# Next pair's input transposes ahead of an overflow conditional, and spilled rows gathered one pair ahead

## The chip, the cores and the metric

The kernel is one program on one core of a Trainium2 chip. The metric is the device time of one execution in microseconds (us); less is better. A core has a matrix engine (TensorE, PE in the rows; PEld is its weight load), VectorE (DVE), ScalarE (ACT), GpSimd (POOL) and SyncE (SP), each with its own instruction stream, and sixteen DMA engines that move data between HBM and on-chip memory. The engines wait for each other through semaphores.

## What is computed

The reference is a two-layer trunk over 512 latent and 256 context tokens of width 1024. Layer 0 mixes tokens with a 2-D Fourier transform and a convolution, layer 1 with two kinds of attention. Each layer ends in a mixture of experts: every token picks one of four groups and in it two of eight experts. Nearly all that the change touches is this part:

```python
def routed_experts(h, e_idx, e_w, w_gate, w_up, w_down):
    ...
    xb = h_pad[row_tok].reshape(n_blocks, EXPERT_BLOCK, d)
    def expert_block(args):
        xblk, e = args
        return (jax.nn.silu(xblk @ w_gate[e]) * (xblk @ w_up[e])) @ w_down[e]
    ...
    return jnp.zeros((n_tok + 1, d), h.dtype).at[row_tok].add(yb * row_w[:, None])[:n_tok]
```

with d = 1024, 32 experts, an expert width of 512, everything in float32. Layer 0 routes 768 tokens (latent and context), layer 1 only the 512 latent ones.

## The kernel before

The program is unrolled: a mixer phase, the experts of layer 0 (`moe`, about 313 to 885 us of the profile), the attention phase, and the experts of layer 1 (about 1266 to 1815 us). In each expert stage all 32 experts are worked off as 16 pairs, in the order ORDER = 0..15.

**A pair.** Each expert of a pair has room for 64 tokens, one half of a 128-row tile. `gather` (L1212) fetches the pair's token rows from HBM into `xg` by an indirect DMA that POOL issues; an index that lies beyond the bound is skipped. `xpose` transposes `xg` on PE (8 instructions, `ps<-cst,xg` in the rows) and ACT and DVE copy the result to `xt`. Then, for the first expert, `gate_up` (16 matmuls of each 4 of the 8 slices, `psg<-ring,mk`), `gated` (Silu on ACT L1338, two products on DVE L1340), `turned` (two transposes, `ps<-cst,hb`), `down` (16 matmuls, `ps<-ring,hb`) and `place` (ACT L1369 copies the result to `y`); the same for the second expert, whose accumulator is `other`. `combine` adds the previous pair's outputs to the stream in between (`ps<-mk,mk`).

**The conditional.** A pair in which an expert got more than 64 tokens needs `overflow` (L1473): behind `tc.If(spills > 0)` stand two inner conditionals (L1477) that run a second half block for one expert from the pair's own `xt`, and one more (L1479) for rows that fit in neither half ("spilled" rows): `spill_gather` (L1381) fetches them into `xs`, and `spill_block`, `spill_split` and `spill_combine` work them off; L1494 is a conditional behind these for still more of them. All engines test the same condition, each in its own stream. An engine that does not enter jumps over the code and then brings its semaphore counters to the values that the others expect; until it has, whoever waits for that engine waits.

**The order around it.** PE's instructions and the weight loads on SP stand in program order by hand. The rest is ordered by the framework's scheduler, which also carries matmuls that are written behind the conditional up ahead of it where nothing forbids that: from the third pair on the `gate_up(other, ..., range(4, 6))` written behind `overflow` stands ahead of the branch.

**The weights.** Six tiles of 2 MB per pair (2048 KB in the rows) go through a ring of eight slots. `load(4)` behind the conditional issues four of them on SP, `load(1)` behind the last `gate_up` of the second expert and `load(1)` behind its `down` one each. A load waits until its slot's last reader on PE is done.

Of the kernel before, what the change touches and what calls it, by code (L numbers as in the profile page):

```python
# [12 lines left out]
ALU = mybir.AluOpType  # L13
# [3 lines left out]
P = 128  # L17
D = 1024
KD = D // P
# [25 lines left out]
ORDER = tuple(range(16))  # L45
# [16 lines left out]
class Kern:  # L62
# [804 lines left out]
    def moe(self, l, segs, outp, rt, last=False):  # L867
        self.turn = 7 - l
        nc, tc, A = self.nc, self.tc, self.A
        V, S, T, G = nc.vector, nc.scalar, nc.tensor, nc.gpsimd  # L870
# [6 lines left out]
        with ExitStack() as es:  # L877
# [333 lines left out]
            def gather(pr_):  # L1211
                return G.indirect_dma_start(  # L1212
                    out=xg, out_offset=None, in_=h2d,
                    in_offset=bass.IndirectOffsetOnAxis(ap=idi[:, pr_:pr_ + 1], axis=0),
                    bounds_check=n, oob_is_err=False)
# [74 lines left out]

            def spill_cols(f, i, pq, w):
                V.tensor_reduce(f[:, 0], pq[:, 0:2 * w].rearrange("p (h e) -> p e h", h=2), axis=AX.X, op=ALU.add)
                V.tensor_copy(i[:, 0], f[:, 0])
                V.tensor_scalar(f[:, 0], f[:, 0], -1.0, None, op0=ALU.add)
                V.tensor_reduce(f[:, 1], third(pq[:, 2 * w:5 * w]), axis=AX.X, op=ALU.add)

# [2 lines left out]
            def spill_table():  # L1299
                spill_cols(sf, si, spill_ids(None, slice(0, 160)), 32)  # L1300
# [30 lines left out]
            def gate_up(po, W, xt, s, ks):  # L1331
                for k in ks:
                    for c in range(2):
                        T.matmul(po[64 * c:64 * c + 64, :], xt[:, k, s], W[0](k // 4)[:, k % 4, c, :], start=k == 0, stop=k == KD - 1)
# [20 lines left out]
            def down(W, ht):  # L1355
                pd = self.ps()
                for j, kt in enumerate((0, 2, 1, 3)):
                    for dh in range(2):
                        T.matmul(pd[64 * dh:64 * dh + 64, :], ht[kt % 2][:, 64 * (kt // 2):64 * (kt // 2) + 64],
                                 W[1]()[:, kt, 512 * dh:512 * dh + 512], start=j == 0, stop=j == 3)  # L1360
                return pd

            def place(dst, i, pd, add=True):
                for dh in range(2):
                    d, p = dst[64 * i:64 * i + 64, 512 * dh:512 * dh + 512], pd[64 * dh:64 * dh + 64, :]
                    if add:
                        V.tensor_tensor(d, p, d, op=ALU.add)  # L1367
                    else:
                        S.activation(d, p, AF.Copy)  # L1369

            def combine(ms, yh, yl, sel):
                for m in ms:
                    pss = [self.ps() for _ in segs]
                    for z, y in enumerate((yh, yl)):
                        for p, (o, w) in zip(pss, segs):
                            T.matmul(p[:, :w], y(m), sel(m)[:, o:o + w], start=z == 0, stop=z == 1)
                    for v, (p, (o, w)) in enumerate(zip(pss, segs)):
                        self.add_gated(m, p, o, w, gate, v)

            def spill_gather(e, ids):  # L1380
                G.indirect_dma_start(  # L1381
                    out=xs[half(e % 2)], out_offset=None, in_=h2d,
                    in_offset=bass.IndirectOffsetOnAxis(ap=ids[0:64], axis=0),
                    bounds_check=n, oob_is_err=False)

            def spill_sel(so, h, idc):
                V.tensor_scalar(so[h], self.cst[h, K_IOTA:K_IOTA + n], idc[h], None, op0=ALU.is_equal)
# [81 lines left out]
            def overflow(pos_, pr_, Ws, xt, y, ys):  # L1469
                shared[0] = {}  # L1470
                if pos_ % 8 == 0:
                    spills[:] = nc.values_load_multi_w_load_instructions(nbi[0:1, 2, 16 + pos_:24 + pos_])[1]
                with tc.If(spills[pos_ % 8] > 0, label=f"ov{l}_{pr_}"):  # L1473
                    tc.mark_branch_hint_location(f"sp{l}_{pr_}", "LikelyTaken", [mybir.EngineType.PE])
                    for i in range(2):
                        e = 2 * pr_ + i
                        with tc.If(value(1, e, None) > 0):  # L1477
                            place(y, 1 - i, extra(Ws[i], xt, half(1 - i), wd[:, 1 - i, e:e + 1]), i == 1)
                    with tc.If(value(3, pr_, None) > 0, label=f"sp{l}_{pr_}"):  # L1479
                        rs_ = [value(0, 2 * pr_ + i, 12) for i in range(2)]  # L1480
                        so = keep([n], F32R, tag="S")
                        for i in range(2):
                            e = 2 * pr_ + i
                            spill_gather(e, si[:, 0, e:e + 1])
                            clear(i, *ys)
                            spill_sel(so, half(i), sf[:, 0, e:e + 1])
                        for i in range(2):
                            e = 2 * pr_ + i
                            with tc.If(rs_[i] > 0):
                                parts = spill_block(Ws[i], e, sf[:, 1, e:e + 1])  # L1490
                                spill_split(e, parts, *ys)
                        spill_combine(slice(0, P), so, *ys)
                        for i in range(2):
                            with tc.If(rs_[i] > 1):  # L1494
                                spill_rest(2 * pr_ + i, Ws[i], rs_[i] - 1, ys)
                shared[0] = None
# [9 lines left out]
            for p, r_ in enumerate(ORDER):  # L1506
                y = keep([D], tag="y3", bufs=3)
                ys = [keep([D], F32R, tag="y3", bufs=3) for _ in range(2)]
                G.memset(y[64:128], 0.0)  # L1509
                W = weights(p)  # L1510
                tc.mark_branch_hint_location(f"ov{l}_{r_}", "LikelyTaken", [mybir.EngineType.PE])
                gate_up(pa, W[0], xt, half(0), range(4, KD))
                h = gated(pa, wd[:, 0, 2 * r_:2 * r_ + 1])
                other = self.bank()
                gate_up(other, W[1], xt, half(1), range(2))
                ht = turned(h)
                if p == 0:
                    spill_table()
                if pend:
                    combine(range(4), *pend)  # L1520
                gate_up(other, W[1], xt, half(1), range(2, 4))
                if pend:
                    combine(range(4, KD), *pend)
                place(y, 0, down(W[0], ht), False)
                overflow(p, r_, W, xt, y, ys)
                load(4)
                if p == 15 and not last:
                    early = []
                    for q in range(2):
                        a = slot()  # L1530
                        for j in range(2):
                            pin(nc.sync.dma_start(out=a[:, 2048 * j:2048 * j + 2048].rearrange("p (k n) -> p k n", k=2), in_=A["modw"][1, 2, 2 * q + j]))
                        early += [a[:, D * k:D * k + D] for k in range(4)]
                gate_up(other, W[1], xt, half(1), range(4, 6))
                own = xt
                if p < 15:
                    xt = xpose(xg, slice(0, P), "xt", 2)
                    if p < 14:
                        gather(ORDER[p + 2])
                gate_up(other, W[1], own, half(1), range(6, KD))  # L1540
                load(1)
                h = gated(other, wd[:, 1, 2 * r_ + 1:2 * r_ + 2])
                if p < 15:
                    pa = self.bank()
                    nw = weights(p + 1)[0]
                    gate_up(pa, nw, xt, half(0), range(2))
                ht = turned(h)
                if p < 15:
                    gate_up(pa, nw, xt, half(0), range(2, 4))
                place(y, 1, down(W[1], ht))  # L1550
                load(1)
                yh, yl = ys
                for q in range(2):
                    cs_ = slice(512 * q, 512 * q + 512)
                    S.activation(yh[:, cs_], y[:, cs_], AF.Copy)  # L1555
                    V.tensor_tensor(yl[:, cs_], y[:, cs_], yh[:, cs_], op=ALU.subtract)  # L1556
                sel = keep([n], F32R, tag="S")
                V.tensor_scalar(sel, self.cst[:, K_IOTA:K_IOTA + n], idf[:, r_:r_ + 1], None, op0=ALU.is_equal)  # L1558
                pend = ((lambda m, a=yh: a[:, mc(m)]), (lambda m, a=yl: a[:, mc(m)]), (lambda m, a=sel: a))
# [135 lines left out]
```

## Time and profile before

| | |
|---|---|
| time, median of 3 runs | 1827.63 us (1825.91 to 1828.39) |
| profiled execution | 1831.84 us, of which the span is 1830.1 us |
| PE busy | 1650.3 us (90%) |
| DVE / ACT / POOL busy | 938.0 / 479.7 / 254.1 us |
| moved by DMA | 507.62 MB, mean 277 GB/s |
| mean granted TensorE clock | 0.958 |

The span runs from the first instruction to the last; the 1.74 us between it and the profiled execution's time lie around it. Engine names with a q (ACTq) are an engine's sequencer: a wait "<-ACTq L1473" ended when ACT's stream had passed the conditional of line 1473. In a row of the timeline the idle time ahead of the instruction stands in brackets, with what ended it. [...]

### The profile page before, as it was taken

The numbers are of one execution on the slowest core, as the hardware profiler recorded it, in microseconds if no ns is written. First come the engines' busy times: TensorE is split into PE (matmuls) and PEld (weight loads), VectorE is DVE, ScalarE is ACT, GpSimd is POOL, SyncE is SP. The second block draws the span as 40 slices with busy tenths as digits, with TensorE's granted clock in tenths as the row PEclk, the third lists the DMA queues.
The fourth block names the chain that finished last, engine by engine and source line by source line (L and its number), as shares of the span: only waits on it lengthen the run. The fifth ranks groups of instructions, "written<-read, shape, count | busy, mean of one in ns | idle before, by whom it ended". The sixth has DMA issues, their size and how long they took to land. (4 is left out here: it accounts for less than half of the span.)

```text
span 1830.1 us, 23551 instructions
## 1 busy us (share of the span) xinstructions
PE 1650.3 (90%) x8877; PEld 915.9 (50%) x8877; DVE 938.0 (51%) x1738; ACT 479.7 (26%) x1044; POOL 254.1 (14%) x200
## 2 busy tenths in 40 slices
PE   6998997989999987999799899997979899999896
PEld 4776785433343433444386778775323333333332
DVE  5799867333353533444555876555223333324235
ACT  4211632111111111111444555342112111111112
POOL 1231343000000010000232201121000000000001
PEclk8999998999999998999999999998999999999998
DMA  8876164778799992999422122376868979989972
GB/s 292 282 241 235 47 276 149 320 315 358 312 418 390 427 353 78 398 425 427 170 65 66 44 87 59 126 269 274 358 275 365 423 324 426 411 346 426 428 306 104
DMA packets 62062, 507.62 MB, mean 277 GB/s; under 512 B 9253, under 2 KB 10933, under 8 KB 35793
## 3 DMA queue, kind: packets, MB, share of 16 engines
q1 hardware_dynamic: 56720, 489.58, 66.7%
q0 software_dynamic: 5056, 14.80, 2.1%
q8 instruction: 111, 1.82, 0.4%
q14 instruction: 175, 1.43, 0.2%
HBM read 501.34 MB, written 7.35 MB: 278 GB/s over the span
## 5 line engine op out<-in xcount | busy, mean ns | idle before, releaser
L55 PE MATMUL psg<-ring,mk 128*64 128x512 f32 x2048 | 492.1, 616 | 3.9 <-DMA ring<-gu 2.5
L293 DVE SCALAR_TENSOR_TENSOR xt<-ps,mod,xt 128x512 f32<-128x512 f32 (+1 forms) x435 | 255.2, 653 | 96.4 <-PE ps L55 73.3
L55 PEld LDWEIGHTS psg<-ring,mk 128*64 128x64 f32 x2048 | 143.3, 141 | 278.4 <-issue 272.9
L55 PE MATMUL ps<-ring,hb 128*64 128x512 f32 x1152 | 261.4, 596 | 1.0
L55 PE MATMUL ps<-mk,mk 128*128 128x512 f32 (+3 forms) x852 | 180.9, 361 | 15.2 <-DVE mk L55 11.3
L1367 DVE TENSOR_TENSOR mk<-ps,mk 64x512 f32<-64x512 f32 x74 | 51.0, 689 | 227.2 <-PE ps L55 213.4
L55 PEld LDWEIGHTS ps<-mk,mk 128*128 128x128 f32 x800 | 130.0, 190 | 52.9 <-DVE xt L293 14.6
L55 PEld LDWEIGHTS ps<-ring,hb 128*64 128x64 f32 x1152 | 79.2, 137 | 153.7 <-issue 147.7
L508 DVE SCALAR_TENSOR_TENSOR cv<-u,convw,cv 128x798 f32<-128x798 f32 x120 | 139.0, 1214 | 3.5 <-ACT cv L506 3.0
L1369 ACT ACTIVATE mk<-ps 64x512 f32<-64x512 f32 x66 | 39.0, 591 | 315.3 <-PE ps L55 305.8
L1212 POOL DMA_INDIRECT xg<-h2d,mk x30 | 30.0, 999 | 598.6 <-PE ps L55 598.6
L55 PE MATMUL ps<-cst,xg 128*128 128x128 f32 x256 | 43.0, 323 | 61.0 <-ACTq L1473 23.5
L1555 ACT ACTIVATE mk<-mk 128x512 fp32r<-128x512 f32 x64 | 40.3, 630 | 186.3 <-DVE mk L1367 184.0
L1558 DVE TENSOR_SCALAR mk<-cst,mk 128x768 fp32r<-128x768 f32 (+1 forms) x32 | 17.7, 554 | 134.6 <-DVEq L1473 73.6
L1509 POOL MEMSET mk<- 64x1024 f32 x32 | 30.3, 946 | 402.9 <-DVE mk L1556 402.8
L1340 DVE SCALAR_TENSOR_TENSOR hb<-hb,mk,psg 128x128 f32<-128x128 f32 x128 | 38.8, 345 | 89.6 <-ACT hb L1338 89.6
L55 PEld LDWEIGHTS ps<-cst,xg 128*128 128x128 f32 x256 | 34.5, 166 | 86.2 <-issue 53.8
L94 POOL TENSOR_TENSOR lo<-wc,hi 128x1024 fp32r<-128x1024 f32 (+3 forms) x25 | 44.4, 1778 | 172.4 <-ACT hi L88 124.4
L110 PE MATMUL ps<-hh,hi 128*128 128x512 f32 (+1 forms) x192 | 59.0, 354 | 8.9 <-ACT hh L283 8.9
L55 PE MATMUL ps<-ring,mk 128*64 128x512 f32 x256 | 60.8, 627 | 5.1 <-PEq L1477 3.0
L1347 ACT ACTIVATE hb<-ps 128x128 f32<-128x128 f32 x144 | 33.5, 276 | 108.3 <-PE ps L55 107.8
L94 POOL TENSOR_TENSOR lo<-wo,hi 128x512 fp32r<-128x512 f32 x32 | 44.6, 1399 | 112.1 <-ACT hi L88 107.7
(370 smaller groups left out, 2516.6 us busy)
## 6 DMA issues: line engine op xcount, KB each, us to landing
ring<-gu SPq DMA_DIRECT2D x125, 2048.0 KB, 19.1
ring<-dn SPq DMA_DIRECT2D x59, 2048.0 KB, 18.6
mw<-modw SPq DMA_DIRECT2D x72, 512.0 KB, 4.7
mw<-modh SPq DMA_DIRECT2D x16, 512.0 KB, 7.5
ring<-dn SPq DMA_DIRECT2D x8, 1024.0 KB, 18.7
wi<-w_in SPq DMA_DIRECT2D x12, 512.0 KB, 6.6
wc<-w_cd SPq DMA_DIRECT2D x11, 512.0 KB, 3.4
h2d<-mk SPq DMA_DIRECT2D x10, 512.0 KB, 2.6
```

The costliest lines, as they stand in the source:

```text
L55: i = f(*a, **k)
L94: nc.gpsimd.tensor_tensor(lo, src, hi, op=ALU.subtract)
L110: T.matmul(o, lh, rh, start=start, stop=False)
L293: self.nc.vector.scalar_tensor_tensor(x, ps[:, :w], g[:, m, v:v + 1], x, op0=ALU.mult, op1=ALU.add)
L508: nc.vector.scalar_tensor_tensor(acc, u[:, j:j + LO], cw[:, j:j + 1], acc, op0=ALU.mult, op1=ALU.add)
L1212: return G.indirect_dma_start(out=xg, out_offset=None, in_=h2d, in_offset=bass.IndirectOffsetOnAxis(ap=idi[:, pr_:pr_ + 1], axis=0), bound ...
L1340: V.scalar_tensor_tensor(h[:, b], h[:, b], wcol, po[:, 256 + P * b:384 + P * b], op0=ALU.mult, op1=ALU.mult)
L1347: S.activation(hb[:, 1, b], po[:, :P], AF.Copy)
L1367: V.tensor_tensor(d, p, d, op=ALU.add)
L1369: S.activation(d, p, AF.Copy)
L1509: G.memset(y[64:128], 0.0)
L1555: S.activation(yh[:, cs_], y[:, cs_], AF.Copy)
```

## The change

The transposes of the next pair's rows, and behind them the gather of the pair after that, are written ahead of `down` and of the conditional; they stood behind it, between two parts of `gate_up(other, ...)`. `own` keeps the current pair's `xt` for the conditional and for the rest of `gate_up`, which is now written in one piece behind it. `spill_gather` leaves the conditional: a new `spill_gathers` issues both gathers of a pair without a condition, one pair ahead (for the first pair behind `spill_table`). `spill_cols` now adds 8192 to a zero index, which puts it beyond the bound, as the table of `gather` already does; that is one more DVE instruction.

```diff
             def spill_cols(f, i, pq, w):
                 V.tensor_reduce(f[:, 0], pq[:, 0:2 * w].rearrange("p (h e) -> p e h", h=2), axis=AX.X, op=ALU.add)
-                V.tensor_copy(i[:, 0], f[:, 0])
+                V.tensor_scalar(f[:, 1], f[:, 0], 0.5, 8192.0, op0=ALU.is_lt, op1=ALU.mult)
+                V.tensor_tensor(i[:, 0], f[:, 1], f[:, 0], op=ALU.add)
...
+            def spill_gathers(r_):
+                for e in (2 * r_, 2 * r_ + 1):
+                    spill_gather(e, si[:, 0, e:e + 1])
...
                             e = 2 * pr_ + i
-                            spill_gather(e, si[:, 0, e:e + 1])
                             clear(i, *ys)
...
                 if p == 0:
                     spill_table()
+                    spill_gathers(ORDER[0])
...
+                own = xt
+                if p < 15:
+                    xt = xpose(xg, slice(0, P), "xt", 2)
+                    if p < 14:
+                        gather(ORDER[p + 2])
                 place(y, 0, down(W[0], ht), False)
-                overflow(p, r_, W, xt, y, ys)
+                overflow(p, r_, W, own, y, ys)
                 load(4)
...
-                gate_up(other, W[1], xt, half(1), range(4, 6))
-                own = xt
                 if p < 15:
-                    xt = xpose(xg, slice(0, P), "xt", 2)
-                    if p < 14:
-                        gather(ORDER[p + 2])
-                gate_up(other, W[1], own, half(1), range(6, KD))
+                    spill_gathers(ORDER[p + 1])
+                gate_up(other, W[1], own, half(1), range(4, KD))
```

How the scheduler places this on PE shows at the fourth pair. One row can stand for several instructions (x4); `ring` is a weight slot, `ps` and `psg` are accumulators, and the body of the conditional is left out. Before, the row ahead of the branch is the half of `gate_up(other)` that was carried up, and behind the conditional come the transposes, the other half, the next pair's first slices, and `turned`:

```order
L55 MATMUL ps_5428<-ring_5264,hb 64x512 x8
L55 MATMUL psg_5349<-ring_5266,mk_5274 64x512 x4
L1473 COMPARE_AND_BRANCH
...
L1690 BRANCH_PREFETCH_HINT
L55 MATMUL ps_6097<-cst,xg 128x128 x4
L55 MATMUL ps_6103<-cst,xg 128x128 x4
L55 MATMUL psg_5349<-ring_5266,mk_5274 64x512 x4
L55 MATMUL psg_6121<-ring_5294,mk_6096 64x512 x4
L55 MATMUL ps_6126<-cst,hb 128x128
```

In the changed kernel the same place on PE reads:

```order
L55 MATMUL ps_5442<-cst,xg 128x128 x4
L55 MATMUL ps_5448<-cst,xg 128x128 x4
L55 MATMUL ps_5457<-ring_5287,hb 64x512 x8
L55 MATMUL psg_5362<-ring_5289,mk_4617 64x512 x8
L1478 COMPARE_AND_BRANCH
...
L1696 BRANCH_PREFETCH_HINT
L55 MATMUL psg_6136<-ring_5307,mk_5441 64x512 x4
L55 MATMUL ps_6141<-cst,hb 128x128
```

The transposes now stand ahead of `down`, the whole rest of `gate_up(other)` ahead of the branch, and behind it only the next pair's first slices are left ahead of `turned`. This holds from the third pair on; in the first two pairs, and in the second pair of layer 1, only three or five of these eight instructions of `gate_up(other)` stand ahead of the branch (the listing counts eight where the profile counts sixteen). On POOL, the rows between the end of one conditional and the next branch are, before:

```order
L1473 UNCONDITIONAL_BRANCH
L1212 DMA xg<-h2d_100,mk_2793 128x1024
L1509 MEMSET mk_6155 64x1024
L1473 COMPARE_AND_BRANCH
L1467 TENSOR_LOAD mk_2851
```

and in the changed kernel:

```order
L1478 UNCONDITIONAL_BRANCH
L1382 DMA xs<-h2d_100,mk_2855 64x1024 x2
L1513 MEMSET mk_6170 64x1024
L1212 DMA xg<-h2d_100,mk_2793 128x1024
L1478 COMPARE_AND_BRANCH
```

Two gathers of 64 rows stand there in every pair, and the gather of `xg` is ahead of the same pair's conditional rather than behind it.

## Rows read from the trace of the kernel before

**Rows 1.** Waits of PE, whole span: releaser, us in total, times, longest.

```profile
PE ps L55 <- ACTq L1473: 23.5, 6, 4.3
PE ps L55 <- DVEq L1479: 20.3, 5, 7.5
PE ps L55 <- DVE hb L1340: 9.4, 10, 1.1
PE ps L55 <- ACTq L1479: 2.2, 1, 2.2
```

**Rows 2.** Groups by line and shape: busy, mean ns, idle before it, releasers.

```profile
L55 PE MATMUL ps<-cst,xg 128*128 128x128 f32 x256 | 43.0, 323 | 61.0 <-ACTq L1473 23.5 <-DVEq L1479 20.3 <-DVEq L1473 8.1
```

**Rows 3.** Timeline around an ordinary pair's branch: start, us, engine, operation, count, idle before.

```profile
753.34 1.89 PE L55 MATMUL psg<-ring,mk 128*64 128x512 f32 x8
756.12 1.07 PE L55 MATMUL ps<-cst,xg 128*128 128x128 f32 x8 [0.89 <-DVEq L1473]
757.12 3.65 PE L55 MATMUL psg<-ring,mk 128*64 128x512 f32 x16
759.16 0.38 ACT L1338 ACTIVATE hb<-psg 128x256 f32<-128x256 f32 x1 [1.77 <-PE psg L55]
759.57 0.61 DVE L1340 SCALAR_TENSOR_TENSOR hb<-hb,mk,psg 128x128 f32<-128x128 f32 x2 [1.66 <-ACT hb L1338]
```

**Rows 4.** Timeline of PE around the branch of a pair where ACT is late.

```profile
1426.58 1.89 PE L55 MATMUL psg<-ring,mk 128*64 128x512 f32 x8
1432.61 1.97 PE L55 MATMUL ps<-cst,xg 128*128 128x128 f32 x8 [4.14 <-ACTq L1473]
1434.51 5.50 PE L55 MATMUL psg<-ring,mk 128*64 128x512 f32 x16
```

**Rows 5.** Busy time by window (PE, PEld, DVE, ACT, POOL), clock, DMA share, GB/s.

```profile
1432.60:1437.00 4.40, 4.39 (x14) 2.34 (x16) 1.37 (x4) 1.50 (x4) 0.99 (x1) 0.50 1.01 430
756.00:760.00 4.00, 3.88 (x22) 1.91 (x24) 1.74 (x4) 0.98 (x2) 1.00 (x1) 1.00 0.94 311
```

**Rows 6.** Timeline of PE: first work behind a branch, and behind two entered conditionals.

```profile
333.23 1.06 PE L55 MATMUL psg<-ring,mk 128*64 128x512 f32 x2 [0.43 <-PEq L1473]
1371.33 1.94 PE L55 MATMUL ps<-cst,xg 128*128 128x128 f32 x8 [7.50 <-DVEq L1479]
1636.66 1.06 PE L55 MATMUL ps<-cst,xg 128*128 128x128 f32 x8 [1.81 <-DVEq L1479]
```

**Rows 7.** The same window view: two long stretches, and two at entered conditionals.

```profile
488.30:685.60 197.30, 184.32 (x866) 80.17 (x868) 84.71 (x158) 28.61 (x67) 17.62 (x18) 0.96 0.97 399
1504.00:1631.00 127.00, 117.91 (x530) 46.08 (x530) 45.94 (x87) 22.97 (x58) 7.77 (x8) 0.97 0.98 408
...
1351.50:1364.90 13.40, 11.31 (x50) 3.53 (x50) 1.61 (x4) 0.94 (x3) 0.00 (x0) 1.00 0.01 3
...
1631.00:1636.00 5.00, 3.74 (x17) 1.06 (x16) 1.09 (x2) 0.42 (x2) 0.00 (x0) 1.00 0.14 29
```

**Rows 8.** Timeline of PE, where it waits for weights in layer 1.

```profile
1697.28 3.33 PE L55 MATMUL psg<-ring,mk 128*64 128x512 f32 x8 [2.48 <-DMA ring<-gu]
```

**Rows 9.** DMA view: packets, MB, share; issues with KB each and us to landing.

```profile
q0 software_dynamic: 5056, 14.80, 2.1%
...
ring<-gu SPq DMA_DIRECT2D x125, 2048.0 KB, 19.1
...
xg<-h2d,mk POOLq DMA_INDIRECT x32, 11.1
```

**Rows 10.** Timeline of the one pair with spilled rows: second gather, first transposes.

```profile
669.33 0.94 POOL L1381 DMA_INDIRECT xs<-h2d,mk  x1 [0.16 <-issue]
678.69 1.08 PE L55 MATMUL ps<-cst,xs 64*128 64x64 f32 x8 [5.81 <-issue]
```

**Rows 11.** Timeline at layer 1's first pair: a gather's issue, and `down` ahead of the branch.

```profile
1268.70 1.06 POOL L1212 DMA_INDIRECT xg<-h2d,mk  x1 [3.73 <-PE ps L55]
1281.79 3.60 PE L55 MATMUL ps<-ring,hb 128*64 128x512 f32 x16
```

## The prediction

> **What bounds the kernel now.** TensorE is busy for 90% of the span, so the first view to read is PE's list of waits [rows 1]. Its two largest entries end with the sequencers of ACT (23.5 us in six waits) and DVE (20.3 us in five), at the conditional. The groups by shape [rows 2] say which instruction pays: the 256 transposes of `xg`, with 61.0 us of idle ahead of them. They are the first PE work behind the branch, and they need an accumulator that ACT or DVE has emptied, so PE stands until that engine has got past its own branch. That is the work which the change takes away from there, and 61.0 us is the ceiling of what the waits can give.
>
> The timeline shows two kinds. In an ordinary pair the last matmuls ahead of the branch end at 755.2 and the transposes start 0.89 us later [rows 3]. In six pairs ACT is late: the wait is 4.14 us [rows 4], and behind it the eight transposes take 1.97 us where the ordinary pair shows 1.07, and the next sixteen matmuls 5.50 where it shows 3.65. [...] In an entered conditional it is DVE that is late, by up to 7.50 us, though elsewhere only by 1.81 [rows 6]; the 20.3 us in five are two of the larger size and three of the smaller.
>
> The window view gives the second bound [rows 7]. Between two entered conditionals the DMA engines are busy for 0.97 to 0.98 of the time at 399 to 408 GB/s, and idle only while PE works in an entered conditional: 0.01 in the 13.4 us up to 1364.9, 0.14 in the 5.0 us up to 1636. From 1504, the end of one entered conditional, to 1636, the end of the next, lie four pairs of six tiles of 2.097 MB, 50.3 MB, which at 408 GB/s take 123 us of the 132. So there TensorE and the weights are nearly even, and PE already waits for a tile once, 2.48 us [rows 8]. What PE saves in such a stretch can only come out of those last few idle microseconds.
>
> **The change, part by part: PE's waits.** In an ACT-late pair ACT is free 6.0 us after `down` (1426.6 to 1432.6) [rows 4]. The changed kernel runs all sixteen matmuls of `gate_up(other)` behind `down` (3.65 us), the branch (0.43, what PE shows where matmuls that need no one follow it [rows 6]), and eight matmuls of the next pair (1.85): it comes to `turned` 5.9 us after `down`. `turned` needs Silu on ACT (0.38) and the first of two products on DVE (0.3) [rows 3], so it can start at 6.0 + 0.7 = 6.7, a wait of 0.8. In place of 4.14 stand 0.43 + 0.8: 2.9 saved, and 2.75 of clock, since no gap stays long: 5.7 us per pair, 34 for six. An entered pair with DVE 7.5 late reaches the same wait after 0.43 + 1.85 and needs 0.7 behind it: 0.43 + 5.9 remain, 1.1 saved, the low clock stays. One with 1.81 keeps about 0.6 and saves 1.2. Seven pairs enter, the five of these DVE waits, one with a wait for ACT [rows 1] and one with spilled rows [rows 10]: about 8 us. The sixteen or so ordinary ones go from some 0.75 to 0.43: 5 us. The waits for `hb` (9.4 us in ten [rows 1]) get the branch as additional cover, some 0.4 each: 4 us. On PE alone this is 34 + 8 + 5 + 4 = 51 us.
>
> **What moves with it.** The transposes (1.07) and the second half of `gate_up(other)` (1.85) now stand ahead of the branch, so within a pair the four loads behind the conditional are issued 2.9 us later. While tiles are queued that costs nothing: a tile lands 19.1 us after its issue [rows 9], against 2.097 MB / 408 GB/s = 5.1 us each, so three to four stand in the queue. But at an entered conditional the queue is empty, and the stream starts again 2.9 us later relative to PE's work. A stretch that the weights pace then grows by up to 2.9 us; one that PE paces does not, since its end moves as its beginning did.
>
> The gather of `xg` needs 11.1 us of a pair of 27 or more [rows 9] and is issued earlier than before; hidden. Only in layer 1's first pair it is short: issued at 1268.70, due at 1281.8 where `down` now follows the transposes [rows 11]. By the median landing it is there at 1279.8, with a landing some 3 us slower it is not: 0 to 2 us, I take 1.
>
> The spilled gather leaves the conditional in one pair only. Its second half was issued at 669.33, and PE's first `xs` transposes start at 678.69 after 5.81 us "issue", which names no DMA [rows 10]: 0 to 5.8 us saved, I take 0.
>
> In return 62 more gathers run, nearly all empty. POOL has 0.94 us for each [rows 10], beside 14% of busy time, and nobody waits for it. On the DMA engines all 5056 packets of that queue took 2.1% of the span, 38 us or 7.6 ns per packet, mostly for rows that move 4 KB [rows 9]. If an empty place cost as much, 62 x 64 would take 30 us of the stream; if it costs nothing, 0. A place beyond the bound moves no row, so I take a value near the lower end, 3.5 us, counted where the weights pace. The extra DVE instruction runs twice per layer: nothing.
>
> **The sum.** The seven entered conditionals cut the program into stretches, and I take each by its slower side. Layer 0: the first three pairs gain nothing (0.43 stands there already [rows 6]); pairs 3 and 4 gain 2.5 with the late DVE ahead of them; the six up to 722.9 have one ACT-late pair, but 0.97 of DMA share: I take 2 lost, between 2.9 lost and 8 gained; the tail gains 2, being 2.9 shorter behind its last branch, once no load is waiting. Layer 1: the first pairs hold an ACT-late one and are followed by 13.4 us of idle DMA, 5.7 less 1 for the gather: 4.5. The next four, with another, I take at 2, the four up to 1636 at 1 lost, the rest, where the wait of 2.48 stands, at 0.5. Together 2.5 - 2 + 2 + 4.5 + 2 - 1 + 0.5 = 8.5 gained; less 3.5 for empty gathers, 5 us. The profiled execution, 1831.84 us, would come to 1827; it lies 4.2 us above the median, and 1827.63 - 5 gives **1823 us**. Most of the 51 us on PE turn into waits for weights.
>
> **Rivals.** *PE's saving comes through.* If the queue has more lead than I give it, each stretch is worth its PE saving up to its idle DMA. For it speaks that the DMA share of whole stretches is under 1; against it the wait in [rows 8], which lies in one of them. Layer 1's four stretches have an ACT-late pair each and could give some 6 us, 5 where the idle time ends at 1636, layer 0's the 0, 2.5, 8 and 6 of their PE waits: 39, less 3.5, so about 1792 us.
>
> *Slower, by DVE at the entered conditionals.* DVE is late by 7.5 us there in one case and by 1.81 in another with the same code [rows 6]. What is behind that branch on PE needs DVE's products now, not only its accumulators. Were DVE late by 7.5 in all seven, the other five would have 6.3 idle in place of some 2, and the low clock behind it: about 7 each, 35; paced stretches hide about half, 17 and more on top of the forecast: 1840 us. It decides once three of the five turn late (some 10 us, against my gain of 5). For it speaks that two of seven are late already; against it that three with 1.81 are not.
>
> [...]
>
> *The wait only moves.* If `turned` waits for ACT and DVE as long as the transposes did, or the weights take back all of it: 1828 us, no change.
>
> **Chances.** Forecast 0.48 (its own range 1814 to 1831), PE's saving 0.15, slower by DVE 0.22, the moved wait 0.15. A measurement of this kernel tells 0.2%, 3.7 us, from no change. Faster: 0.29 of the forecast and all but 0.01 of the first rival, 0.43; same: 0.14 and 0.13, 0.27; slower: 0.05, 0.22 and 0.03, 0.30. The range reaches half way to the first rival and over the second: 1806 to 1841.
>
> **What would show it.** The idle ahead of the transposes should fall from 61.0 to under 10 us, and a wait ahead of `turned` (`ps<-cst,hb`) should grow from 9.4 to some 25. Waits of PE for `ring` should grow from 2.48 us to 15 or more, with a DMA share of 0.98 or above in the long stretches; if they stay small, the first rival holds. In ACT-late pairs the clock behind the branch should read 1.00. If more than two entered conditionals show over 5 us ahead of `turned`, the second rival is at work. If waits for weights grow while the rate falls below 399 to 408 GB/s, I priced the empty gathers too low.

## The result, and the profile after

The changed kernel takes 1849.01 us (1848.54 to 1849.53), the kernel before 1827.53 us beside it: a ratio of 1.0119, 95% interval 1.0101 to 1.0136. It is 21.5 us slower, where 5 us faster was forecast; the measured time lies above the range, beyond the second rival's 1840 us. The profiled execution has a span of 1847.3 us against 1830.1.

The wait that the change takes away is gone. The groups by shape of the changed kernel (busy, mean ns of one, idle before, releasers) put 2.4 us ahead of the transposes of `xg`, where [rows 2] had 61.0, and they run at 282 ns each in place of 323. ACT's sequencer, 23.5 us in [rows 1], is no longer among PE's releasers:

```profile
L55 PE MATMUL psg<-ring,mk 128*64 128x512 f32 x2048 | 497.2, 620 | 48.0 <-DMA ring<-gu 35.7 <-PEq L1484 5.6 <-PEq L1478 5.6
...
L55 PE MATMUL ps<-cst,hb 128*128 128x128 f32 x144 | 35.7, 322 | 40.5 <-DVE hb L1341 40.5
...
L55 PE MATMUL ps<-cst,xg 128*128 128x128 f32 x256 | 35.0, 282 | 2.4 <-DMA xg<-h2d,mk 2.4
```

Two other waits have taken its place, as PE's list of waits over the whole span shows (releaser, us in total, times, longest):

```profile
PE ps L55 <- DVE hb L1341: 40.5, 17, 6.0
PE psg L55 <- DMA ring<-gu: 35.7, 13, 4.6
...
PE ps L55 <- PEq L1482: 7.1, 5, 2.8
PE psg L55 <- PEq L1484: 5.6, 6, 1.7
PE psg L55 <- PEq L1478: 5.6, 12, 0.6
```

Ahead of `turned` PE waits 40.5 us for DVE's products (9.4 before, [rows 1]), and 35.7 us for weight tiles, where [rows 8] was the one wait of that kind. The first is not spread over the pairs. The timeline of PE has five long ones, and each lies behind an entered conditional: once in layer 0 (422.46) and at all four in layer 1. Three of them:

```profile
422.46 0.79 PE L55 MATMUL ps<-cst,hb 128*128 128x128 f32 x2 [5.99 <-DVE hb L1341]
...
1372.37 0.73 PE L55 MATMUL ps<-cst,hb 128*128 128x128 f32 x2 [5.93 <-DVE hb L1341]
...
1511.13 0.73 PE L55 MATMUL ps<-cst,hb 128*128 128x128 f32 x2 [5.74 <-DVE hb L1341]
```

(The other two, 5.88 at 1649.01 and 5.96 at 1787.69, read the same.) Of these five, two had shown a late DVE before (7.37 at 413.86, and the 7.50 of [rows 6]); the other three are the places that showed 1.81. They make up 29.5 of the 40.5 us.

DVE's own timeline at the third one says what it did. It finished its last work ahead of the jump at 1504.1, then stood for 6.12 us until its sequencer was past the conditional of line 1484, and only then made the products:

```profile
1502.69 1.39 DVE L1368 TENSOR_TENSOR mk<-ps,mk 64x512 f32<-64x512 f32 x2 [4.19 <-PE ps L55]
1510.21 0.48 DVE L1564 TENSOR_SCALAR mk<-cst,mk 128x512 fp32r<-128x512 f32 x1 [6.12 <-DVEq L1484]
1510.72 0.60 DVE L1341 SCALAR_TENSOR_TENSOR hb<-hb,mk,psg 128x128 f32<-128x128 f32 x2
```

The DMA view of 1503.3 to 1509.7, nearly all of that stretch, has one packet on an instruction queue, of 0.01 MB:

```profile
q14 instruction: 1, 0.01, 0.3%
```

Such packets come at other times too. But at all seven late places, five here and two in the kernel before, one stands 2.3 us ahead of the moment at which DVE goes on, within its wait; at the three places where DVE was early before, none stands in the 0.52 us of its wait. The view does not say which engine a packet is for. The weights went on arriving meanwhile, with their queue at 92.8% of the engines' time.

And the clock falls behind such a wait, and behind a long wait for weights too. The window view (last columns: granted clock, DMA share, GB/s) has 0.50 in both; the eight matmuls that follow take 3.68 us, against 1.94 at a granted 1.00 behind a wait of 0.81 (1503.45 to 1505.39):

```profile
1511.00:1514.00 3.00, 2.87 (x8) 1.14 (x10) 0.33 (x2) 0.56 (x2) 0.00 (x0) 0.50 1.04 434
1460.00:1465.00 5.00, 4.65 (x12) 1.45 (x14) 0.00 (x0) 0.52 (x2) 0.00 (x0) 0.50 1.01 426
```

```profile
1460.35 3.68 PE L55 MATMUL psg<-ring,mk 128*64 128x512 f32 x8 [4.60 <-DMA ring<-gu]
```

### The profile page after: what moved, and what is told of

Read it like the earlier page. It is cut to its first block, busy times and chain, and to the rows that moved or that the text cites. A ratio compares the mean times of both kernels' runs of the same rounds, so it can differ in the third digit from the quotient of the medians.

```text
span 1847.3 us, 23616 instructions
## 1 busy us (share of the span) xinstructions
PE 1651.0 (89%) x8877; PEld 915.7 (50%) x8877; DVE 933.2 (51%) x1740; ACT 481.4 (26%) x1044; POOL 317.6 (17%) x262
## 2 busy tenths in 40 slices
DMA packets 67020, 507.50 MB, mean 275 GB/s; under 512 B 14240, under 2 KB 15920, under 8 KB 40752
## 3 DMA queue, kind: packets, MB, share of 16 engines
HBM read 517.59 MB, written 7.35 MB: 284 GB/s over the span
## 5 line engine op out<-in xcount | busy, mean ns | idle before, releaser
L55 PE MATMUL psg<-ring,mk 128*64 128x512 f32 x2048 | 497.2, 620 | 48.0 <-DMA ring<-gu 35.7
L1382 POOL DMA_INDIRECT xs<-h2d,mk x64 | 64.3, 1005 | 360.7 <-PEq L1478 148.8
L1339 ACT ACTIVATE hb<-psg 128x256 f32<-128x256 f32 x64 | 24.6, 384 | 192.7 <-PE psg L55 64.6
L55 PE MATMUL ps<-cst,hb 128*128 128x128 f32 x144 | 35.7, 322 | 40.5 <-DVE hb L1341 40.5
L55 PEld LDWEIGHTS ps<-cst,hb 128*128 128x128 f32 x144 | 16.5, 145 | 106.1 <-DVE hb L1341 84.6
## 6 DMA issues: line engine op xcount, KB each, us to landing
ring<-dn SPq DMA_DIRECT2D x8, 1024.0 KB, 20.3
```

The lines of the kernel that those rows point to most:

```text
L55: i = f(*a, **k)
L1382: G.indirect_dma_start(out=xs[half(e % 2)], out_offset=None, in_=h2d, in_offset=bass.IndirectOffsetOnAxis(ap=ids[0:64], axis=0), bounds_ch ...
```

## Experiments

Three theories stood against each other: the loss is DVE's lateness behind entered conditionals, which depends on how DVE's code lies (theory 1); the 62 nearly empty gathers slow the weights (theory 2); or the move itself loses, because loads are issued later (theory 3). The text under each kernel is what was written before it ran. Ratios are to the kernel before on the same chip, with 95% intervals.

### The two halves of the change alone

`transposes_only` keeps the spilled gathers in the conditional and the old index table; of the diff it has

```diff
+                own = xt
+                if p < 15:
+                    xt = xpose(xg, slice(0, P), "xt", 2)
+                    if p < 14:
+                        gather(ORDER[p + 2])
                 place(y, 0, down(W[0], ht), False)
-                overflow(p, r_, W, xt, y, ys)
+                overflow(p, r_, W, own, y, ys)
```

> Only the transposes and the gather of xg move ahead of the conditional; the spilled gathers stay inside it and the index table is as before. Theory 1 (DVE late behind entered conditionals, where its code happens to lie): the time follows the number of entered pairs with more than 5 us ahead of turned, 1849 us with five of them, some 5 us less for each one fewer, so 1832 to 1836 with two. Theory 2 (the 62 nearly empty gathers slow the weights): about 1829 us whatever DVE does. Theory 3 (the move itself, by loads issued 2.9 us later): 1847 to 1850 us, as with the whole change.

`gathers_only` has the other half: the index table, `spill_gathers` and its two calls.

> Only the spilled gathers leave the conditional; the transposes stay behind it. Theory 2 (gathers slow the weights): the loss is here, 1843 us or more, with waits of PE for ring tiles. Theories 1 and 3: 1824 to 1831 us where two entered conditionals show DVE late by 7.5 us ahead of the transposes, and some 5 us more for each further one.

Measured: `transposes_only` 1833.46 us, 1.0033 (1.0013 to 1.0054); `gathers_only` 1850.41 us, 1.0128 (1.0090 to 1.0165). By that alone the gathers would be the culprit, and theory 2 would hold. But the waits of `gathers_only` tell another story. PE waits for weights 1.9 us, less than before; what has grown is the wait for DVE behind entered conditionals, 36.8 us in five, all of them long, against 20.3 in five before ([rows 1]), two of them long:

```profile
PE ps L55 <- DVEq L1484: 36.8, 5, 7.6
...
PE ps L55 <- ACTq L1478: 18.5, 6, 3.6
...
PE psg L55 <- DMA ring<-gu: 1.9, 1, 1.9
```

At the third of the three places shown above the kernel before had waited 1.81 us (first line); `gathers_only` waits 7.47 (second). Changed there are the length of DVE's code and the place of POOL's gathers:

```profile
1504.82 1.06 PE L55 MATMUL ps<-cst,xg 128*128 128x128 f32 x8 [1.81 <-DVEq L1479]
...
1509.31 1.94 PE L55 MATMUL ps<-cst,xg 128*128 128x128 f32 x8 [7.47 <-DVEq L1484]
```

In `transposes_only` the long waits stand at the same two places as before (the one in layer 0 is 5.88 us at 420.23). So the late places seem to follow the index table, one DVE instruction more in `spill_cols`, which is written out 66 times in the program, nearly always in parts that are not entered. The table without the gathers was not run by itself; with a shift of 64 beside it, it does change the late places, as shown below. Theory 3 is not dead either: with the same two places late as before, `transposes_only` is 6 us slower than the kernel before, clear of the noise. In the pair with spilled rows PE now waits for the gather inside the conditional: the gather of `xg` stands ahead of it on POOL. But before, PE had waited at the same place as well, 5.81 us without a named end ([rows 10]), and in the changed kernel, where that gather has long been issued, 4.62 us are left (second line):

```profile
687.78 1.09 PE L55 MATMUL ps<-cst,xs 64*128 64x64 f32 x8 [6.48 <-DMA xs<-h2d,mk]
...
689.57 1.08 PE L55 MATMUL ps<-cst,xs 64*128 64x64 f32 x8 [4.62 <-issue]
```

### Moving DVE's code without adding work

`changed_dve_shift64` is the changed kernel with this in the spilled part of layer 0's first pair, which no engine enters:

```diff
                         rs_ = [value(0, 2 * pr_ + i, 12) for i in range(2)]
+                        if l == 0 and pos_ == 0:
+                            shift = keep([1], tag="shift")
+                            for _ in range(64):
+                                V.memset(shift, 0.0)
```

> The changed kernel with 64 one-element memsets on DVE written into the spilled part of layer 0's first pair, which no engine enters: no work is added, but all of DVE's code behind it lies 64 instructions later. Theory 1: the entered pairs in which DVE is late are other ones; if three of layer 1's four become early, the waits of PE for hb fall from 40.5 to some 23 us and the time to 1832 to 1837 us. Theories 2 and 3: 1847 to 1851 us, as the changed kernel.

Measured: 1816.70 us, 0.9939 (0.9921 to 0.9957). A kernel that executes the same work is 32 us faster than the changed one, and faster than the kernel before. That is outside the ranges of all three theories, since all five late places became early and not three. It was run twice more beside others: 1820.32 us, 0.9957 (0.9938 to 0.9975), and 1818.25 us, 0.9951 (0.9931 to 0.9970).

> The same kernel as changed_dve_shift64, timed again beside the others of this group: 1814 to 1820 us, with DVE early behind all entered conditionals.

DVE is early behind all entered conditionals. At the same conditional as above its sequencer is past the jump 0.52 us after the last work in place of 6.12, and no wait stands ahead of `turned`:

```profile
1490.85 1.39 DVE L1368 TENSOR_TENSOR mk<-ps,mk 64x512 f32<-64x512 f32 x2 [4.19 <-PE ps L55]
1492.76 0.49 DVE L1568 TENSOR_SCALAR mk<-cst,mk 128x512 fp32r<-128x512 f32 x1 [0.52 <-DVEq L1484]
```

```profile
1491.61 1.94 PE L55 MATMUL psg<-ring,mk 128*64 128x512 f32 x8 [0.81 <-PEq L1484]
1493.68 0.59 PE L55 MATMUL ps<-cst,hb 128*128 128x128 f32 x2
```

The whole list of this kernel has 11.4 us for `hb` (40.5 in the changed one), but more for weights, not less:

```profile
PE psg L55 <- DMA ring<-gu: 45.6, 15, 6.5
...
PE ps L55 <- DVE hb L1341: 11.4, 13, 1.4
```

So theory 1 holds for most of the loss. By the ratios the five late places are worth 30 to 33 us, some 6 each, and the changed kernel has three more of them than the kernel before: by that price 18 to 20 of the 21.5 us. This share is an estimate, for the price is not the same everywhere: `gathers_only` with its three more late places is 23 us slower than the kernel before, some 8 each.

With DVE early the weights do pace these stretches. Between two entered conditionals of layer 1 the DMA engines are busy for 0.97 of the time in the changed kernel (first line) and for all of it in the shifted one (second):

```profile
1513.00:1628.00 115.00, 107.51 (x484) 42.64 (x480) 43.37 (x81) 21.66 (x53) 13.78 (x14) 0.97 0.97 405
...
1494.00:1610.00 116.00, 104.47 (x468) 41.83 (x469) 43.40 (x81) 21.09 (x53) 13.76 (x14) 0.94 1.01 425
```

Does a shift also cure the kernel before? The same memsets, 96, 64 and 32 of them:

> The kernel before with 96 one-element memsets on DVE in the spilled part of layer 0's first pair, which no engine enters. If DVE is early behind all entered conditionals, the two waits of 7.4 and 7.5 us ahead of the transposes shrink to about 1.8, with the low clock behind them gone. Theory 1 (where DVE's code lies was all of the loss): 1812 to 1818 us, and the change itself is then worth nothing against 1816.7. A rival (the change is worth its saved waits once DVE is early in both): 1826 to 1829 us, since the weights pace and hide the shorter waits.

> The kernel before with DVE's code moved by 64 in a part that is not entered. If DVE becomes early behind the two entered conditionals where it was late: 1812 to 1818 us, and the change is worth nothing at equal lateness; if more become late, 5 to 7 us more than 1828 for each; if the same two stay, 1826 to 1830 us.

> The kernel before with DVE's code moved by 32 in the same place, the same three cases as with 64: 1812 to 1818 us with DVE early everywhere, 1826 to 1830 us with the same two late, 5 to 7 us more for each further one.

Measured: 1828.61 us, 0.9999 (0.9987 to 1.0011); 1826.79 us, 1.0002 (0.9984 to 1.0020); 1826.46 us, 0.9993 (0.9978 to 1.0008). The waits stay as they were, 20.0 or 20.1 us in five with a longest of 7.3 or 7.4: the same two places are late in all three. `transposes_only` with a shift of 96 kept its two late places as well, at 1834.95 us, 1.0056 (1.0036 to 1.0075).

> Only the transposes ahead of the conditional, with DVE's code moved by 96 instructions in a part that is not entered. It differs from the shifted changed kernel (1816.7 us) by the gathers alone. If the gathers' place is worth the 6.5 us that PE waited for xs in the pair with spilled rows: 1820 to 1824 us. If the nearly empty gathers cost the weights more than that: below 1814 us.

For the kernel before, this is the case in which the same two places stay late; the last kernel meets neither of its two ranges, and is 10 us slower than the kernel before at equal late places. It is a limit of theory 1 too: 64 instructions cured the changed kernel, and none of three shifts moved a late place here. By what rule the place of the code decides, or whether it does so alone, these runs do not show.

### The four combinations with an early DVE

What the moves are worth by themselves needs kernels in which DVE is equally late. These give the kernel before and each half of the change the changed kernel's index table and the shift of 64, so that DVE's stream is nearly as long in all four.

> The kernel before with the changed kernel's index table (one more DVE instruction, the padded index) and DVE's code moved by 64 in a part that is not entered. If DVE is early behind all entered conditionals, as it is in the changed kernel with the same shift, the two waits of 7.4 us go. Theory 1 (DVE's lateness was all of the difference): 1815 to 1820 us, level with changed_shift64_again (1820.3). A rival (the moves have a worth of their own once DVE is early): 1825 to 1829 us.

> Only the gathers ahead, with DVE's code moved by 64. With DVE early everywhere the 1850 us of gathers_only fall by 5 to 7 us for each of five late pairs: 1815 to 1825 us; level with before_early_dve if nearly empty gathers cost nothing.

> Only the transposes ahead, with the changed kernel's index table and DVE's code moved by 64. Against changed_shift64_third it lacks the early gathers: if the 6.5 us in which PE waited for xs is their worth, 3 to 6 us slower than that, 1822 to 1826 us; if not, level.

> The whole change with DVE's code moved by 64, beside the other three on the same chip: 1815 to 1821 us.

| moved | us, median | ratio to before (95% interval) | long DVE waits left |
|---|---|---|---|
| nothing (`before_early_dve`) | 1822.92 | 0.9967 (0.9955 to 0.9979) | one, 7.4 |
| gathers (`gathers_early_dve`) | 1822.76 | 0.9975 (0.9960 to 0.9989) | one, 4.2 |
| transposes (`transposes_early_dve`) | 1813.88 | 0.9922 (0.9900 to 0.9944) | none |
| both (`changed_shift64_third`) | 1818.25 | 0.9951 (0.9931 to 0.9970) | none |

`before_early_dve` differs from `before_dve_shift64` by the index table alone, and one of the two late places is gone (14.6 us of waits in five for 20.1): the table does change where DVE is late. With one late place fewer than before, the old order gains 0.33%, 5 to 6 us. Against it the transposes are worth 9 us, of which one late place is about 5 to 6: an estimate of 3 to 4 us for the move where DVE is early. It does not hold where DVE is late: against `transposes_only` the 20 us of difference (1.0033 to 0.9922) would make it 10 for each of two late places, and there the move loses 6. Why a late place costs more in the new order is open. The row has the lowest time of the four. The intervals of the last two rows overlap a little, so that the gathers cost 4 us on top of the transposes is likely, not shown; in the old order no cost shows, with a late place that is 3 us shorter. The 3 to 6 us that the expectation gave the gathers for ending the wait for `xs` are not there. That wait is 5.90 us in `transposes_early_dve`; with the gathers ahead PE's longest wait for something that the profile does not name, 4.62 us at this place in the changed kernel, is still 4.4 in `changed_dve_shift64`: some 1.5 us are gained.

### The price of the empty gathers

`changed_shift64_gathers_twice` issues each unconditional gather twice (`for e in (2 * r_, 2 * r_ + 1) * 2`); `changed_shift64_needed_gathers` issues them for the one pair alone that has spilled rows (`if p == 9 and l == 0:` ahead of the call), so it leaves out 62 gathers that move next to nothing.

> The changed kernel with DVE's code moved by 64, and every unconditional spilled gather issued twice: 64 more gathers, nearly all empty. If an empty gather costs nothing: 1816 to 1818 us. At the price taken in the prediction (3.5 us for 62): 1819 to 1822 us. If empty places cost the weight stream as much as a mean packet: 1830 us or more.

> The changed kernel with DVE's code moved by 64 and the spilled gathers issued, still ahead and without a condition, for the one pair that has spilled rows alone; the 62 nearly empty ones are left out, POOL's memsets and all else stay. If an empty gather costs what doubling them cost (11 us for 64): 1804 to 1808 us. At the price of the prediction (3.5 us): 1811 to 1815 us. If it costs nothing: as changed_shift64_again within 2 us.

Measured: twice 1827.67 us, 1.0013 (0.9996 to 1.0030); only the needed ones 1818.43 us, 0.9961 (0.9944 to 0.9979), beside 1820.32 for all of them. Leaving out 62 is worth 2 us by the medians, inside the noise; but PE's longest wait for `hb` was 2.5 us there, 1.3 in the kernel beside it, so it can be some 1 us more. Adding 64 cost 7 to 11. The DMA view of the changed kernel bounds the price from the engines' side: 4960 packets more than in [rows 9] raise the queue's share from 2.1 to 2.4% of the span, some 6 us of sixteen engines.

```profile
q0 software_dynamic: 10016, 14.71, 2.4%
```

So the first 62 cost 0 to 6 us. The profile's count of bytes read from HBM rises with them, from 501.34 to 517.59 MB, which is 4096 bytes for each of 62 x 64 places, while the bytes that DMA moved do not (507.62 and 507.50 MB). Why the second 64 cost more is open; waits for weights were 49.0 us there, against 43 to 46.

### More cover ahead of `turned`

`changed_more_cover` puts `gate_up(pa, nw, xt, half(0), range(4))` ahead of `turned` in place of `range(2)` and leaves the later call out.

> The changed kernel with all four first slices of the next pair's gate_up ahead of turned rather than two; they read the same weight tile. Theory 1: behind a late DVE the wait ahead of turned is 1.85 us shorter in five pairs, 9 us in all, and the low clock behind it rarer: 1838 to 1842 us. Theory 2 and 3: the wait for hb shrinks but waits for ring tiles grow by as much: 1846 to 1850 us.

> The changed kernel with DVE's code moved by 64 and all four first slices of the next pair ahead of turned. With DVE early the wait for hb is 11 us already, most of it inside the conditional, so the cover can save little: 1814 to 1817 us. If the weights pace all of it: 1816 to 1818 us.

Measured: with DVE late 1841.77 us, 1.0071 (1.0044 to 1.0098), 7 us better than the changed kernel, as theory 1 had it. With DVE early 1833.06 us, 1.0038 (1.0025 to 1.0052), 13 to 16 us worse than without the cover. The second was not expected. Its waits for weights are 51.9 us in 28 against 43.2 to 45.6 in 14 or 15, which is about half of the loss. `turned` comes eight matmuls later, `down` and the load behind it have as many matmuls ahead of them as before. The cause is open.

## Why the prediction was wrong

**The step that failed** is the term for the entered conditionals. The prediction took DVE's lateness as it stood in the trace of before, two places of 7.5 us among the seven, saved 8 us there, and gave the other case 0.22. With it failed "The extra DVE instruction runs twice per layer: nothing". It runs twice in all, not per layer (1740 DVE instructions for 1738), and DVE was not busier for it (933.2 us for 938.0), but it lengthens DVE's code, and no term of the sum had that. Five places were late. The wait at each was priced right: 0.43 and 5.9 in the working, 0.70 to 0.81 and 5.7 to 6.0 where it occurred, with the low clock behind it. The second rival has the mechanism, but hid half of the price behind the weights and stopped at 1840. Less was hidden. The five waits are 29.5 us, and the low clock behind them some 11 (eight matmuls in 3.68 us for 1.94 each time, and a little in those that follow); waits for weights are 8 to 10 us shorter than in the shifted kernel, and the time is 30 to 33 longer. By this estimate about a quarter came back.

What would have helped is that a jump after which PE waited 1.81 us in three cases and 7.50 in another, with the same code, had to be read as a coin that the change throws again, since `spill_cols` changes the length of DVE's stream. The sum kept the old count. The runs agree with that reading in part: a packet on the instruction queue stands 2.3 us ahead of each late return, 64 instructions more took all five late places from the changed kernel, and the index table took one of two from the kernel before with a shift of 64. Three shifts that moved nothing in the kernel before neither bear it out nor refute it; what decides, no view shows.

**The waits at the transposes** went as worked out: 61.0 to 2.4 us, ACT's 23.5 to nothing, eight transposes in 1.03 to 1.09 us in all but the first pair of each layer. No wait for ACT's sequencer is left on PE; `gate_up(other)` covers it. The 2.75 us of clock that the sum gave each ACT-late pair are the 0.90 and 1.85 by which eight transposes and sixteen matmuls take longer in [rows 4] than in [rows 3], at a granted 0.50 against 1.00 ([rows 5]); in the changed kernel the clock behind the branch is 1.00 in five of these six pairs, and in the sixth 0.50 behind a wait of 4.15 us for weights (1736.57). In the kernel before one of the six, at 1727.00, had paid less: 1.09 us for the eight transposes behind a wait of 3.90, and 5.35 for the sixteen matmuls.

**The weights** took back about what was forecast: of 51 us on PE the sum kept 8.5, and 35.7 us of waits for weights were measured, in pieces of up to 4.6 ("15 or more" was the sign). What the working did not have is that such a wait can cost twice: behind the six of 3.76 us or more the granted clock was 0.50 to 0.57 and eight matmuls took 3.34 to 3.68 us, behind the seven of up to 2.31 they took 1.94. [rows 8] had shown it, 3.33 us for eight behind a wait of 2.48, at a clock of 0.56. The other sign, a DMA share of 0.98 or above, is there with DVE early (1.01, waits of 43 to 46 us) and not in the changed kernel (0.97). The rate did not fall below 399 GB/s in either.

**The small terms** held. The late `xg` gather in layer 1's first pair cost 1.88 us (0 to 2 given, 1 taken). The empty gathers cost 0 to 6 us (3.5 taken). The spilled gather's move saved about 1 us, 4.62 in place of 5.81 (0 taken); with the transposes moved that gather would have been waited for by name, which the working missed, and that is worth 1.5.

**As a whole**, that PE's gain is mostly lost to the weights is right. The gain of 5 that should have been left does not show at equal lateness. By the group of four the old order with its last late place taken off comes to some 1817 us, an estimate, against 1818.25 for the whole change; and with the two late places of before, the transposes alone lost 6 us, 10 with a shift of 96. Why they lose there is open. That the shifted change is 8 to 11 us faster than the kernel before, near the 5 forecast, is luck, since it lacks the two late places that the kernel before has. The sign of the measured result came from the second rival's mechanism.

## What to carry to other kernels

Behind a conditional that an engine jumps over, look at how long each engine takes to get past it, place by place. If the same code shows 0.5 us here and 6 there, treat the count of late places as something that any edit may change, in either direction, and compare variants at equal lateness before crediting or blaming the edit; here a variant that only moved code by 64 instructions, which no engine enters, differed by 1.6 to 1.8%. Where two resources are nearly even, count a removed wait as gained only up to the slack of the other one, and price the wait that replaces it with the low clock seen behind it, 0.50 to 0.57 here behind the longer waits for DVE and for weights.

## What the runs showed of the hardware

- A taken jump over the spilled part let DVE go on after 0.52 us (`changed_dve_shift64`) or after 6.12 us (the changed kernel), for the same work; 64 instructions more in a part that is never entered turned all five late places early in the changed kernel, while 32, 64 or 96 more changed none in the kernel before. What decides it is open.
- At each of the seven late places of the kernel before and the changed one, a packet on an instruction queue stands 2.3 us ahead of DVE's return; at the three early places of the kernel before none stands in the 0.52 us of DVE's wait.
- 62 gathers whose places lie nearly all beyond the bound put 4960 packets more on their queue and raised its share of the span from 2.1 to 2.4%. The count of bytes read from HBM rose by 4096 for each place, 16.25 MB, while the bytes moved stayed at 507.5 MB.
- Behind a wait of 5.74 us for DVE and behind one of 4.60 us for weights the granted clock was 0.50; behind 0.81 us it was 1.00, and eight matmuls took 1.94 us in place of 3.68.
